# Low parts of attention's query and key weights from a negated cast and an accumulating DMA

## The chip, the cores and the metric

The kernel runs on one core of one Trainium2 chip. The metric is the device time of one execution in microseconds (us). Three runs of the kernel before took 949.86, 948.94 and 949.84 us, a median of 949.84 us. The profile is one further execution; its times count from the start of its span.

Engine names in the profile: PE is TensorE (matrix multiplications), PEld its weight loads, DVE is VectorE, ACT is ScalarE, POOL is GpSimd, SP is SyncE, which issues most of the loads here.

## What is computed

A decoder trunk of two layers on 512 tokens of 1024 features in float32. Layer 0 mixes tokens by pooling, layer 1 by causal differential attention; each is followed by a gated feed-forward network, and a normalisation stands behind every part:

```python
for i in range(DEPTH):
    if i % N_MIXERS == 0:
        h = _multiscale_pool(x, pool_w[j], pool_scale[j])
    else:
        h = _diff_attention(x, w_qkv[j], w_o[j], lam_p[j], subln_g[j], rel_table, lambda_init)
    x = _layernorm(ALPHA * x + h, ln_mix_g[i], ln_mix_b[i])
    x = _layernorm(ALPHA * x + _swiglu(x, w_gate[i], w_up[i], w_down[i]), ln_ffn_g[i], ln_ffn_b[i])
```

The change lies in the attention of layer 1, which has eight heads of two 64-wide halves:

```python
qkv = x @ w_qkv
...
s = jnp.einsum('bhcqd,bhckd->bhcqk', q[...], k[...]) * sm_scale
...
p = jax.nn.softmax(s, axis=-1)
a = p[:, :, 0] - lam * p[:, :, 1]
outs.append(jnp.einsum('bhqk,bhkv->bhqv', a, v[...]))
```

## The kernel before

**Two parts for each operand.** TensorE multiplies in a format called fp32r, which keeps fewer bits than float32. So each operand is held as two tiles: a high part h, the value cast to fp32r, and a low part l, the value minus h. A product takes three multiplications: high by high, high by low, low by high (`mm3`, line 125). `split` (line 102) makes the two parts: a cast on ACT (line 109) and a subtraction on DVE (line 110), or on POOL where the caller asks for it.

**The weight stream.** All weights lie in one array `wall` in HBM, cut into pieces of 128x1024 float32 (512 KB) in the order in which they are used. `fetch` (line 95) has SP load a piece into one of five buffers, `raw`. `ready(upto)` (line 112) brings the stream forward: for each next piece c it first asks for the loads up to piece c + 4, then takes a pair of tiles `w{c}h`, `w{c}l` out of six pairs and splits `raw` into them. The load of piece c + 4 reuses the buffer of piece c - 1, so it waits until nobody reads that one any more. `weights` and `take` hand finished pairs to the multiplications.

**The attention pieces.** Pieces 68 to 91 belong to queries, keys and values. Every pair of heads has six: two of values (`v`, 68 and 69 for heads 0 and 1), then query and key of the even head (70, 71), then query and key of the odd head (72, 73). So w76 and w77 are query and key of head 2, w78 and w79 of head 3, w82 and w83 of head 4, w88 and w89 of head 6. Pieces 92 to 99 are the output projection.

**The order of a head.** The order of all work is written out by hand (line 241): each engine runs its instructions in the order of the program, and waits only for data and for buffers to be free. Head h goes as follows (lines 1183 to 1231). TensorE makes the values (`values`); DVE finishes the previous head's softmax (`combine`, lines 1104 to 1109); `ready` splits pieces up to this head's key; the values are split into `vh`, `vl`; an earlier head's output is scaled (`root`, `scaled`). Then `ready` moves one piece on, TensorE makes the queries, ACT and DVE split them (`heads`, lines 104 and 105), TensorE transposes the previous head's probabilities and makes the keys; `ready` moves on, the keys are split (lines 109 and 110), `ready` moves on again, and `mix` multiplies the previous head's probabilities by its values. ACT squares that result (`sq`, line 1145) and casts the square; POOL subtracts (`sql`). Last come the four score blocks (line 1085), for each of which DVE adds the bias and takes the minimum (line 1090, an accumulator read follows) and ACT takes the exponential (line 1095). The scores are done by TensorE in one go; the next head's values follow them.

So a piece that `ready` splits is, on ACT and DVE, queued between the instructions of the head that calls it: in the odd heads 1, 3 and 5 the query piece of the next head is the last thing before `sq` on ACT and before line 1090 on DVE; in head 0 the key piece of head 1 (w73) and a value piece (w74) are. The key pieces of heads 2, 4 and 6 are split at the start of their own head.

**DMA queues.** SP issues the loads of the weight stream. POOL issues none in attention; in the feed-forward stages it issues plain loads (line 665) and loads that add to what is in the destination (line 666, `accum_op`).

Of the kernel before, what the change touches and what calls it, by code (L numbers as in the profile page):

```python
# [13 lines left out]
F32R = mybir.dt.float32r  # L14
BF16 = mybir.dt.bfloat16
AF = mybir.ActivationFunctionType
ALU = mybir.AluOpType
# [8 lines left out]
FB = FF // P  # L26
HEADS = 8
# [27 lines left out]
def trunk(ctx, tc, x, wall, pscale, lam_p, subln, table, lng, lnb, band, first, onehot, out):  # L55
    nc = tc.nc
# [18 lines left out]
    def weight_pair(name):  # L75
        return tuple(
            keep.tile([P, 1024], F32R, tag=f"w{q}", name=f"{name}{q}", bufs=WBUFS) for q in "hl"
        )
# [11 lines left out]
    raws = {}  # L90
    fetched = [0]
    divided = [0]
    total = wall.shape[0]

    def fetch(upto):
        while fetched[0] < min(upto, total):
            c = fetched[0]
            raws[c] = keep.tile([P, 1024], F32, tag="raw", name=f"raw{c}", bufs=RAWS)
            nc.sync.dma_start(out=raws[c], in_=wall[c])
            fetched[0] += 1  # L100

    def split(dst_h, dst_l, src, scale=1.0, low=None):
        if scale != 1.0:
            nc.scalar.mul(dst_h, src, scale)
            nc.vector.scalar_tensor_tensor(
                dst_l, src, scale, dst_h.bitcast(F32), op0=ALU.mult, op1=ALU.subtract
            )
        else:
            nc.scalar.copy(dst_h, src)  # L109
            (low or nc.vector).tensor_tensor(dst_l, src, dst_h.bitcast(F32), op=ALU.subtract)  # L110

    def ready(upto, low=None):
        while divided[0] < min(upto, total):
            c = divided[0]
            fetch(c + RAWS)
            h, l = weight_pair(f"w{c}")
            split(h, l, raws.pop(c), low=low)
            parts[c] = (h, l)
            divided[0] += 1

    def weights(c):
        ready(c + 1)
        return parts[c]
# [118 lines left out]
    with tc.tile_pool(name="pool", bufs=1) as pp:  # L242
# [161 lines left out]
        mixed(0, 1)  # L404
        mixed(1, 0, 1)
        ready(3, nc.gpsimd)
        summed(0, 0)
        split_pooled(1, 0, 1)
# [24 lines left out]
        spread_of(0, 2)  # L433
        turned(0, 1)
        ready(4)
        summed(3, 0, 1)
        norm(0, 2)
# [939 lines left out]
```

## Time and profile before

| what | value |
|---|---|
| median of three runs | 949.84 us (948.94 to 949.86) |
| span of the profiled execution | 947.3 us |
| that execution's own time | not given apart from its span |
| attention in the span | about 383 to 600 us |
| TensorE's granted clock in attention | 1.00 |
| one key or query piece: cast on ACT, subtraction on DVE | 1.05 us, 1.22 us |

How to read the lines that follow. A row of the timeline gives the start and length in us, the engine, the line of the kernel, the operation, what it writes and reads with shapes, and in brackets how long the engine stood idle before it and what ended that. A row of the waits view gives who waited for whom, the total in us, how often, and the longest. A row by tile or line gives the count, the shortest, median and longest time of one in ns, and the first and last start in us. The row of a window gives its length, then busy time (and count) of PE, PEld, DVE, ACT and POOL, then the granted clock, the busy share of the DMA engines and GB/s. The chain row gives the share of the span by engine in the chain of work that ended last.

### The profile page before, as it was taken

Reading aid. Unit: us, or ns where it says so; the run is one execution under the profiler, and the core shown is the slowest. Engines: PE = TensorE matmul, PEld = TensorE weight load, DVE = VectorE, ACT = ScalarE, POOL = GpSimd, SP = SyncE. Lnnn points to the kernel's source line nnn. Section 1 sums busy time; section 2 is a strip of 40 time slices with the busy share of each in tenths; the row PEclk is TensorE's granted clock in tenths of the full one; section 3 lists DMA queues with packets and bytes.
Section 4 is the critical chain, followed back from the end, with each engine's and each line's share of the span. In section 5 each row is a group of like instructions: output and inputs, shape, how many; then the busy total and the mean of one; then the engine's idle time right before and its main releaser. Section 6 shows DMA issues by size and latency. Waiting matters only on the chain.

```text
span 947.3 us, 15363 instructions
## 1 busy us (share of the span) xinstructions
PE 934.1 (99%) x5976; PEld 845.7 (89%) x5976; DVE 781.3 (82%) x1149; ACT 490.1 (52%) x788; POOL 108.4 (11%) x133
## 2 busy tenths in 40 slices
PE   9999999999999999999999999999999999999996
PEld 8898899999988888988888888998899999988885
DVE  8859879999988777688777677789779999987778
ACT  6752444555564457655566553833345554564450
POOL 4121121110001101000000000211111110001101
PEclk9999999999999999999999999999999999999998
DMA  9387988885888964333233222396888885878952
GB/s 244 125 266 236 341 269 246 265 261 208 255 255 271 363 219 136 95 89 101 78 123 83 64 90 90 118 324 197 262 266 250 255 272 204 261 249 271 356 171 90
DMA packets 82248, 196.99 MB, mean 208 GB/s; under 512 B 14804, under 2 KB 26324, under 8 KB 82174
## 3 DMA queue, kind: packets, MB, share of 16 engines
q1 hardware_dynamic: 42876, 115.07, 36.9%
q0 software_dynamic: 15520, 46.14, 17.8%
q10 hardware_dynamic: 23778, 34.78, 10.2%
q8 instruction: 47, 0.77, 0.3%
q14 instruction: 27, 0.22, 0.1%
HBM read 159.25 MB, written 36.72 MB: 207 GB/s over the span
## 4 chain that ended last, share of the span: by engine, by line
PE 92%; DVE 4%; ACT 2%; issue 1%; POOL 0%; DVEq 0%; POOLq 0%
PE A L820 17%; PE P L886 13%; PE C L820 9%; PE Q L886 6%; PE B L820 4%; PE g L129 3%; PE u L128 3%; PE u L127 3%; PE u L129 3%; PE g L127 3%; PE g L128 3%; PE s L1085 2%; PE v L127 2%; PE v L128 2%; PE v L129 2%; PE q L128 2%
## 5 line engine op out<-in xcount | busy, mean ns | idle before, releaser
L566 DVE TENSOR_TENSOR raw<-raw,raw 128x1024 f32<-128x1024 f32 x56 | 68.3, 1219 | 0.5
L109 ACT CAST xs<-hid 128x512 fp32r<-128x512 f32 (+1 forms) x60 | 34.7, 581 | 24.4 <-DVE hid L734 24.4
L224 ACT ACTIVATE y<-pt,bT,gT 128x128 f32<-128x128 f32 x96 | 36.1, 456 | 20.1 <-PE pt L213 20.1
L110 DVE TENSOR_TENSOR xs<-hid,xs 128x512 fp32r<-128x512 f32 (+1 forms) x60 | 38.5, 644 | 7.8 <-ACT xs L109 7.8
L1095 ACT ACTIVATE p<-p,mn 128x128 f32<-128x128 f32 (+3 forms) x64 | 35.4, 554 | 14.9 <-DVE mn L1090 14.9
L665 POOL DMA_DIRECT2D b<-in_wall x20 | 14.0, 705 | 175.0 <-DVE g_58l L572 66.1
L598 DVE TENSOR_TENSOR hid<-sg,u 128x512 f32<-128x512 f32 x16 | 11.0, 687 | 27.5 <-PE u L129 16.8
L726 POOL DMA_DIRECT2D xs<-ssum x24 | 17.4, 725 | 140.7 <-PE Q L886 119.5
L177 POOL TENSOR_TENSOR rs<-rs,mhalf 128x1 f32<-128x1 f32 x16 | 12.5, 784 | 170.5 <-DVE rs L176 131.0
L110 DVE TENSOR_TENSOR xt<-y,xt 128x512 fp32r<-128x512 f32 x24 | 16.3, 689 | 17.5 <-ACT xt L109 17.5
L1090 DVE CUSTOM_DVE_ANT_0 p<-s,bias 128x128 f32<-128x128 f32 (+3 forms) x64 | 28.1, 485 | 0.0
L665 POOL DMA_DIRECT2D hid<-in_wall x24 | 18.7, 821 | 81.1 <-DMA tsum<-hid 49.4
L110 POOL TENSOR_TENSOR sql<-sq,sqh 128x512 fp32r<-128x512 f32 x7 | 9.0, 1291 | 165.3 <-ACT sqh L109 165.3
L702 ACT CAST v<-u 128x512 fp32r<-128x512 f32 x22 | 13.6, 620 | 26.9 <-DVE u L700 26.7
L168 DVE BATCH_NORM_STATS2 st<-res 128x6 f32<-128x512 f32 x32 | 22.2, 695 | 1.1
L846 ACT ACTIVATE sg<-sg 128x512 f32<-128x512 f32 x14 | 8.9, 633 | 25.7 <-DVE sg L839 25.7
L110 DVE TENSOR_TENSOR heads<-k,heads 128x512 fp32r<-128x512 f32 x8 | 5.5, 692 | 19.9 <-ACT heads L109 19.9
L614 ACT CAST xs<-hid 128x1024 fp32r<-128x1024 f32 x8 | 8.4, 1051 | 24.0 <-DVE hid L631 11.6
L666 POOL DMA_DIRECT2D hid<-in_wall x12 | 14.8, 1232 | 48.2 <-DMA hid<-in_wall 44.9
L835 DVE TENSOR_TENSOR hid<-C,hid 128x512 f32<-128x512 f32 x14 | 9.7, 692 | 10.8 <-PE C L820 9.2
L1109 DVE SCALAR_TENSOR_TENSOR p<-p,sm,p 128x128 f32<-128x128 f32 (+3 forms) x32 | 17.7, 552 | 1.1
L109 ACT CAST heads<-k 128x512 fp32r<-128x512 f32 x8 | 4.7, 589 | 26.0 <-PE k L129 26.0
(1119 smaller groups left out, 3727.7 us busy)
## 6 DMA issues: line engine op xcount, KB each, us to landing
raw<-in_wall SPq DMA_DIRECT2D x122, 512.0 KB, 4.5
r<-tsum SPq DMA_DIRECT2D x40, 512.0 KB, 4.3
hid<-in_wall POOLq DMA_DIRECT2D x36, 512.0 KB, 6.9
b<-in_wall POOLq DMA_DIRECT2D x30, 512.0 KB, 6.4
r<-in_wall SPq DMA_DIRECT2D x30, 512.0 KB, 4.5
tsum<-hid ACTq DMA_DIRECT2D x24, 512.0 KB, 5.3
ssum<-v ACTq DMA_DIRECT2D x22, 512.0 KB, 4.4
tsum<-b ACTq DMA_DIRECT2D x20, 512.0 KB, 5.2
```

The source lines that it names most:

```text
L109: nc.scalar.copy(dst_h, src)
L110: (low or nc.vector).tensor_tensor(dst_l, src, dst_h.bitcast(F32), op=ALU.subtract)
L127: nc.tensor.matmul(acc, ah, bh, start=start, stop=False)
L128: nc.tensor.matmul(acc, ah, bl, start=False, stop=False)
L129: nc.tensor.matmul(acc, al, bh, start=False, stop=stop)
L224: nc.scalar.activation(y[:, k, :], pt[:, k * P : (k + 1) * P], AF.Identity, bias=bT[:, n, kk : kk + 1], scale=gT[:, n, kk : kk + 1],)
L566: tt(t, raws[pair[0]], raws[pair[1]], op=ALU.add)
L665: nc.gpsimd.dma_start(out=t[:, j], in_=src[:, j])
L820: nc.tensor.matmul(o, w[:, c], x[:, kk, :], start=p in ("P1", "Q5", "P2") and f + kk + e == 0, stop=p in ("Q4", "Q3", "P2") and (f, kk, e) ...
L886: nc.tensor.matmul(accs[s], x[:, k, r], y[:, c], start=first and k == 0 and e == 0, stop=last and k == m - 1 and e == 2, skip_group_check= ...
L1090: nc.vector.tensor_tensor_reduce(out=p, in0=accs[c][:, :w], in1=biases[h][:, w - 1 :: -1] if w < S else biases[h][:, ::-1], op0=ALU.add, o ...
L1095: nc.scalar.activation(p, p, AF.Exp, bias=mn[:, q, c : c + 1], scale=-1.0, accum_out=sm[:, q, c : c + 1],)
```

## The change

For the query and key pieces of heads 1 to 7 (14 pieces: 72, 73, 76 to 79, 82 to 85, 88 to 91) the low part is made in another way. ACT casts the raw piece to the high tile as before; then ACT writes the negated cast of the raw piece into the low tile; then POOL issues a DMA that reads the same piece from `wall` in HBM once more and adds it to the low tile. The result is again the value minus its high part. DVE does nothing for these pieces. All other pieces go through `split` as before.

```diff
+    attn = 2 + 3 * FB
+    by_dma = {attn + 6 * (h // 2) + 2 + 2 * (h % 2) + i for h in range(1, HEADS) for i in range(2)}
...
             h, l = weight_pair(f"w{c}")
-            split(h, l, raws.pop(c), low=low)
+            raw = raws.pop(c)
+            if c in by_dma:
+                nc.scalar.copy(h, raw)
+                nc.scalar.mul(l, raw, -1.0)
+                nc.gpsimd.dma_start(out=l, in_=wall[c].bitcast(F32R), accum_op=ALU.add)
+            else:
+                split(h, l, raw, low=low)
             parts[c] = (h, l)
```

## The prediction, made before the changed kernel was run

> **What bounds the kernel now.** I read the page's totals first, then the chain that ended last, then the attention stage alone (383 to 600 us from the span's start: one row of the windows view, then the waits inside it).
>
> ```profile
> span 947.3 us, 15363 instructions
> PE 934.1 (99%) x5976; PEld 845.7 (89%) x5976; DVE 781.3 (82%) x1149; ACT 490.1 (52%) x788; POOL 108.4 (11%) x133
> PE 92%; DVE 4%; ACT 2%; issue 1%; POOL 0%; DVEq 0%; POOLq 0%
> ```
> ```profile
> 383.00:600.00 217.00, 216.77 (x1335) 188.92 (x1334) 163.68 (x360) 124.44 (x274) 10.52 (x9) 1.00 0.29 89
> ```
> ```profile
> ACT heads L109 <- PE k L129: 26.0, 8, 3.8
> ...
> PEld v L127 <- DVE mn L1090: 2.1, 6, 0.4
> ```
>
> TensorE carries 92% of the chain. In attention (the columns are length, then busy time of PE, PEld, DVE, ACT, POOL, then granted clock, DMA share, GB/s) it is busy for 216.8 of 217 us at clock 1.00, DVE for 75%, ACT for 57%, and the DMA engines for 29%. So time taken from DVE is worth only what TensorE waits for DVE here: six waits, 2.1 us together, each for the accumulator read of the fourth softmax pass (line 1090) behind a head's scores. More can be lost: every operand that arrives late stops an engine that now hardly stops.
>
> **What the change removes.** For 14 pieces (query and key, heads 1 to 7) the subtraction on DVE goes: 14 x 1.23 us = 17.2 us (row 415.03 below), taking DVE in this stage from 163.7 to 146.5 us. The prices are in these rows of head 1 and the start of head 2 (engine ACT, then DVE, then PEld, each in order of time):
>
> ```profile
> 413.94 1.05 ACT L109 CAST w76h<-raw 128x1024 fp32r<-128x1024 f32 x1
> 415.33 0.60 ACT L1145 ACTIVATE sq<-o 128x512 f32<-128x512 f32 x1 [0.33 <-PE o L129]
> ...
> 422.49 1.03 ACT L109 CAST w77h<-raw 128x1024 fp32r<-128x1024 f32 x1
> 423.44 0.59 ACT L109 CAST vh<-v 128x512 fp32r<-128x512 f32 x1
> ```
> ```profile
> 415.03 1.23 DVE L110 TENSOR_TENSOR w76l<-raw,w76h 128x1024 fp32r<-128x1024 f32 x1 [0.26 <-ACT w76h L109]
> 416.17 0.28 DVE L1090 CUSTOM_DVE_ANT_0 p<-s,bias 128x128 f32<-128x128 f32 x1
> ...
> 417.28 0.08 DVE L1090 DVE_READ_ACCUMULATOR2_ANT mn<- 128x1 f32 x1
> 417.41 0.17 DVE L1104 RECIPROCAL sm<-sm 128x2 f32<-128x2 f32 x1
> ...
> 423.00 0.55 DVE L1105 TENSOR_SCALAR p<-p,sm,nlam 128x512 f32<-128x512 f32 x1
> ```
> ```profile
> 417.40 0.19 PEld L127 LDWEIGHTS v<-w74h,xt 128*128 128x128 f32 x1 [0.35 <-DVE mn L1090]
> ```
>
> In the odd heads 1, 3 and 5 the removed subtraction (w76, w82, w88) stands just ahead of the first softmax pass: it ends at 416.26 and the pass starts at 416.17, when its scores are already being made. Without it the pass waits for its scores alone. The wait behind it is 0.35 us, so the gain per odd head lies between 0 and 0.35; I take 0.3, nearly the whole wait, since DVE would then be free from 414.77 on (415.03 less the 0.26 it stood idle). In the even heads the piece at that place is a value piece, which stays on DVE, so nothing changes there. Gain: 3 x 0.3 = 0.9 us.
>
> **What it adds on ACT.** 14 negated casts of the same shape as the cast ahead of them, 1.05 us each: 14.7 us, ACT 124.4 to 139.1 of 217 us. From start to next start such a cast costs ACT 0.95 us (422.49 to 423.44). Most lie ahead of a wait of ACT for TensorE (26.0 us over eight heads ahead of the key's cast), which hides them; without that cover each would hold what follows it on ACT by 0.95. Behind w76 the cover is short: cast at 413.94, negated cast 414.89 to 415.94, so sq starts at 415.84, not 415.33: 0.5 later. The exponentials behind sq, the reciprocal (417.41) that waits for them, the later softmax passes and with them w77's cast follow 0.5 later. TensorE waits for none of these in this head.
>
> In head 0 there is no cover:
>
> ```profile
> 393.58 1.05 ACT L109 CAST w73h<-raw 128x1024 fp32r<-128x1024 f32 x1
> 394.52 1.05 ACT L109 CAST w74h<-raw 128x1024 fp32r<-128x1024 f32 x1
> ```
> ```profile
> 395.80 1.22 DVE L110 TENSOR_TENSOR w74l<-raw,w74h 128x1024 fp32r<-128x1024 f32 x1
> 396.94 0.28 DVE L1090 CUSTOM_DVE_ANT_0 p<-s,bias 128x128 f32<-128x128 f32 x1
> ...
> 398.05 0.09 DVE L1090 DVE_READ_ACCUMULATOR2_ANT mn<- 128x1 f32 x1
> ```
> ```profile
> 398.18 0.19 PEld L127 LDWEIGHTS v<-w68h,xt 128*128 128x128 f32 x1 [0.37 <-issue]
> ```
>
> The negated cast of w73 goes between the two casts: w74h starts at 395.46 and ends at 396.51, and w74's subtraction, freed of w73's ahead of it, still starts only at 396.55, 0.75 later than 395.80. The softmax passes behind it move by as much, and the values' first weight load at 398.18 follows the fourth accumulator read (398.05 + 0.09) as it does in head 1 (417.36, then 417.40). The view puts this wait to issue, but the distance is the same. Loss: 0.75 us, with 0 as its other end should that wait not be DVE's.
>
> **What it adds on POOL and the DMA engines.** 14 accumulating transfers of 512 KB, issued by POOL. Nothing accumulates in attention now, so the landing L is bounded by the transfers of line 666 (accumulating) and line 665 (plain, same size and queue) in the feed-forward stages. First line 666 whole, then its one transfer at 688.4, then line 665; then the DMA share around 688 and where the new ones will run; then the plain loads in attention.
>
> ```profile
> L666 POOL DMA_DIRECT2D hid<-in_wall x12: 1222/1230/1243, 55.1 to 748.6; - x12
> ...
> DMA to landing us min/median/max: 5.8/6.9/10.8
> ```
> ```profile
> L666 POOL DMA_DIRECT2D b<-in_wall x1: 1227/1227/1227, 688.4 to 688.4; - x1
> ...
> DMA to landing us min/median/max: 6.0/6.0/6.0
> ```
> ```profile
> DMA to landing us min/median/max: 4.2/6.4/10.5
> ```
> ```profile
> 688.00:695.00 7.00, 7.00 (x42) 6.20 (x41) 3.98 (x6) 0.72 (x2) 1.23 (x1) 1.00 0.93 261
> ...
> 425.00:431.00 6.00, 6.00 (x34) 5.07 (x33) 5.02 (x7) 2.13 (x4) 0.00 (x0) 1.00 0.24 87
> ```
> ```profile
> raw<-in_wall SPq DMA_DIRECT2D x31, 512.0 KB, 3.6
> ```
>
> L lies between 4.2 (as quick as the quickest plain one) and 10.8 (the slowest accumulating one). The engines are at 0.24 where w77's will run, so I go by the quick end of the accumulating rows, 5.8 to 6.0, and take 6.0: SP's next raw load waits for the same negated cast to free its buffer, so it runs beside the accumulation (3.6 us from issue to landing). POOL's queue: the next instruction behind such a DMA is the subtraction of sql, which waits for ACT anyway and is read a head later; an issue of 1.23 us there costs nothing. Destination and source are fp32r here and f32 in line 666; no row has that form, and the upper end stands for it.
>
> A rule of the Trainium skill (DMA: Bandwidth & Descriptors, Anatomy of one DMA) puts a POOL-issued transfer at 2.0 us plus bytes over 436 GB/s, an estimate of 3.2 us for 512 KB. The rows disagree, 4.2 for the quickest plain and 5.8 for the quickest accumulating one. By the rule nothing below would be late and the sum would be that of the second case.
>
> **What becomes late.** The rows give the first weight load of a low part. The key pieces of the even heads, w77, w83 and w89, are the tight ones, cast at the head's beginning and used some 8 us later; of the other eleven the queries of the same heads, w76 first, have the least time.
>
> ```profile
> L129 PEld LDWEIGHTS q<-xt,w76l x8: 187/188/188, 423.9 to 428.7; 128*128 128x128 f32 x8
> ```
> ```profile
> L129 PEld LDWEIGHTS k<-xt,w77l x8: 187/188/188, 430.5 to 435.3; 128*128 128x128 f32 x8
> ```
> ```profile
> 458.92 1.05 ACT L109 CAST w82h<-raw 128x1024 fp32r<-128x1024 f32 x1
> 460.70 0.60 ACT L1145 ACTIVATE sq<-o 128x512 f32<-128x512 f32 x1 [0.72 <-PE o L129]
> ...
> 467.86 1.03 ACT L109 CAST w83h<-raw 128x1024 fp32r<-128x1024 f32 x1
> ```
> ```profile
> L129 PEld LDWEIGHTS k<-xt,w83l x8: 187/188/188, 475.5 to 480.3; 128*128 128x128 f32 x8
> ```
> ```profile
> 503.92 1.05 ACT L109 CAST w88h<-raw 128x1024 fp32r<-128x1024 f32 x1
> 505.42 0.60 ACT L1145 ACTIVATE sq<-o 128x512 f32<-128x512 f32 x1 [0.45 <-PE o L129]
> ...
> 512.59 1.03 ACT L109 CAST w89h<-raw 128x1024 fp32r<-128x1024 f32 x1
> ```
> ```profile
> L129 PEld LDWEIGHTS k<-xt,w89l x8: 187/187/188, 520.5 to 525.3; 128*128 128x128 f32 x8
> ```
>
> w77: cast at 422.49 + 0.51 = 423.00, negated cast 423.95 to 424.99, POOL issues at 425.04, landing at 431.04, and 0.05 for the semaphore: 431.09. TensorE wants it at 430.5, or 430.2 once it has gained 0.3 ahead: it waits 0.9. w83: sq 0.12 late by the rows of w82, cast at 467.98, negated cast 468.93 to 469.97, landing at 476.07 with the semaphore, wanted at 475.2: 0.9. w89: sq 0.40 late, cast at 512.99, POOL issues at 515.03, landing with the semaphore at 521.08, wanted at 520.2: 0.9. Where L is below 5.1 none waits; above, each waits L - 5.1. w76, issued at 415.99 and wanted at 423.6, is late only if L is over 7.6, and what TensorE waits there the key behind it no longer does, since its own issue does not move. The stall moves everything behind it, so nothing else becomes late.
>
> **Sum**, on the profiled execution: 0.75 + 3 x (0.9 - 0.3) = +2.55 us, span 947.3 to 949.85. The median of the runs shown, 949.84, is 2.54 above the span, and that part stays: **952.4 us**. In general the sum is 0.75 + 3 x (max(0, L - 5.1) - 0.3).
>
> **The rivals.**
>
> *The accumulation lands in time* (L at most 5.1): no stall, 0.75 - 0.9 = -0.15, 949.7. For it: the quickest plain one took 4.2 at the same queue, and attention's DMA engines are mostly idle. Against it: none of 22 accumulating ones took under 5.8.
>
> *The accumulation is slow* (fp32r destination, or the raw load beside it): at L = 8.5, between median and maximum, 0.75 + 3 x 3.1 = +10, 959.9; at 10.8, 966.8. For it: the accumulations at 6.9 and above stood beside other loads, as these will. Against it: the share of 0.24.
>
> *DVE's relief decides, and it is faster.* Place: the waits behind the scores. Were all six of them to vanish (2.1 us) and head 0's 0.37 as well, -2.5, 947.3. It decides only if L is under 5.1 and head 0's values do not wait for w74; against it stands that three of the six have a value piece ahead, which the change leaves on DVE.
>
> A rule of the Trainium skill speaks against the change (SBUF — State Buffer, Who interferes with whom): while DVE runs a `tensor_scalar` in its two-port mode, POOL cannot write the descriptors of its DMAs. Were each of the three late transfers to meet the longest such instruction here (line 1105, 0.55 us), the sum would be 3 x 0.55 higher, 954.0. I leave it out: moved by the same 0.5, that instruction ends at 424.06, a microsecond before POOL issues, and the 22 issues of line 666 kept to about 1.23 us.
>
> **How the numbers follow.** The forecast (L from 5.2 to 7.0) has 0.47, with its own range 950.0 to 955.4; in time 0.20; slow 0.26; faster 0.07. Below 948.9 only the faster case lies; the slow case reaches 961 at L = 8.9, above which I leave some 0.1. Range 948.9 to 961. A measurement of this kernel tells about 0.2% from no change, 1.9 us: faster 0.07; within, the second case and the forecast's share with L under 5.8, 0.29; slower 0.64.
>
> **What would show it.** Right: in the changed trace TensorE waits for a DMA at the low parts w77l, w83l and w89l by some 0.9 us each; head 0's wait behind the scores grows from 0.37 to 1.1; the waits of heads 1, 3 and 5 shrink to under 0.1; ACT's sq of head 1 starts later than TensorE's o allows; accumulating landings near 6.0. Wrong: landings under 5 or over 8, waits at query pieces (then L is over 7.6), TensorE waiting for ACT at the scores, or a difference outside 383 to 560 us.

## The result, and the profile after

The changed kernel took 955.0 us (median of four, 954.39 to 956.14) where the kernel before, beside it, took 949.7: a ratio of 1.006, 95% interval 1.0045 to 1.0074, or 5.3 us more. The forecast was 952.4 us, in a range of 948.9 to 961, and slower with a chance of 0.64. The direction held, and so did three of the four places; the size that was forecast was half of what came. The two profiled executions are 6.3 us apart (spans of 947.3 and 953.6 us), 1 us more than the medians. A ratio here is taken over all the runs, so it need not be the quotient of the two medians.

First the totals and the chain of the changed kernel's page, then its attention stage in one row of the windows view (columns as before).

```profile
span 953.6 us, 15383 instructions
...
PE 935.9 (98%) x5976; PEld 846.1 (89%) x5976; DVE 765.7 (80%) x1135; ACT 503.3 (53%) x802; POOL 120.8 (13%) x147
...
PE 86%; DVE 5%; issue 3%; ACT 2%; DMA 2%; POOL 1%; DVEq 0%; POOLq 0%; ACTq 0%
```
```profile
383.00:600.00 217.00, 212.29 (x1311) 184.15 (x1310) 142.98 (x341) 132.63 (x278) 22.72 (x23) 1.00 0.47 121
```

DVE's busy time in the span fell by 15.6 us, as it was meant to (781.3 to 765.7), ACT's rose by 13.2. TensorE, busy for 216.8 us of this stage before, is now busy for 212.3 of the same 217: the stage has got holes. DMA stands in the chain for the first time, with 2%. Where the holes are, the waits view of the changed kernel from 383 to 560 us tells (who waited for whom, total, times, longest):

```profile
DVE p L1098 <- PE s L1093: 3.4, 3, 1.2
...
PEld k L137 <- DMA w89l<-in_wall: 2.8, 1, 2.8
...
PEld v L135 <- DVE mn L1098: 2.2, 6, 0.4
...
PEld k L137 <- DMA w77l<-in_wall: 1.6, 1, 1.6
...
PEld k L137 <- DMA w83l<-in_wall: 1.0, 1, 1.0
...
PEld s L1093 <- DVE mn L1098: 0.8, 1, 0.8
```

Four waits are new: the key pieces w77l, w83l and w89l, 5.4 us together, and head 0's scores, 0.8. That is 6.2 of the 6.3 us between the two spans. The three keys are where the prediction had them; in head 0 it had the wait at the values. The six waits at v (2.2 us) stand as they stood before (2.1). Line numbers are 8 higher from `weights` on; line 122 is the negated cast, line 123 the accumulating DMA.

The landings in the same stage of the changed kernel (issues view, the last column is the median us from issue to landing):

```profile
raw<-in_wall SPq DMA_DIRECT2D x30, 512.0 KB, 4.2
...
w77l<-in_wall POOLq DMA_DIRECT2D x1, 512.0 KB, 6.6
...
w83l<-in_wall POOLq DMA_DIRECT2D x1, 512.0 KB, 6.1
...
w89l<-in_wall POOLq DMA_DIRECT2D x1, 512.0 KB, 7.9
```

Before the change a raw load landed after 3.6 us here, now after 4.2: beside the new transfers the raw loads are slower.

How one of these pieces goes, in the timelines of ACT, POOL and PEld of the changed kernel:

```profile
425.45 1.05 ACT L122 ACTIVATE w77l<-raw 128x1024 fp32r<-128x1024 f32 x1
```
```profile
426.80 0.88 POOL L123 DMA_DIRECT2D w77l<-in_wall  x1 [6.83 <-ACT w77l L122]
```
```profile
431.71 0.19 PEld L136 LDWEIGHTS k<-xt,w77h 128*128 128x128 f32 x1
433.46 0.19 PEld L137 LDWEIGHTS k<-xt,w77l 128*128 128x128 f32 x1 [1.55 <-DMA w77l<-in_wall]
```

The negated cast ends at 426.50, POOL issues 0.30 later, the transfer lands 6.6 after that at 433.4, and the first weight load that needs it starts at 433.46, having been due at 431.91.

### The profile page after: what moved, and what is told of

The parts are those of the page before. It is cut to its first block, busy times and chain, and to the rows that moved or that the text cites. A ratio compares the mean times of both kernels' runs of the same rounds, so it can differ in the third digit from the quotient of the medians.

```text
span 953.6 us, 15383 instructions
## 1 busy us (share of the span) xinstructions
PE 935.9 (98%) x5976; PEld 846.1 (89%) x5976; DVE 765.7 (80%) x1135; ACT 503.3 (53%) x802; POOL 120.8 (13%) x147
## 4 chain that ended last, share of the span: by engine, by line
PE 86%; DVE 5%; issue 3%; ACT 2%; DMA 2%; POOL 1%; DVEq 0%; POOLq 0%; ACTq 0%
PE A L828 17%; PE P L894 13%; PE C L828 8%; PE Q L894 6%; PE B L828 4%; PE g L137 3%; PE u L136 3%; PE u L135 3%; PE u L137 3%; PE g L136 3%; PE g L135 3%; PE k L137 2%; PE k L135 1%; PE k L136 1%; PE s L1093 1%
## 5 line engine op out<-in xcount | busy, mean ns | idle before, releaser
L1103 ACT ACTIVATE p<-p,mn 128x128 f32<-128x128 f32 (+3 forms) x64 | 35.4, 555 | 14.7 <-DVE mn L1098 14.7
L1093 PE MATMUL s<-heads 64*128 64x256 f32 (+2 forms) x192 | 18.2, 330 | 0.4 <-DVE mn L1098 0.4
L843 DVE TENSOR_TENSOR hid<-C,hid 128x512 f32<-128x512 f32 x14 | 9.7, 691 | 10.8 <-PE C L828 9.3
```

Source lines behind the costliest of these rows:

```text
L1103: nc.scalar.activation(p, p, AF.Exp, bias=mn[:, q, c : c + 1], scale=-1.0, accum_out=sm[:, q, c : c + 1],)
```

## The experiments

Theory A: three key pieces arrive late and head 0's scores wait behind w74; the other ten pieces cost nothing. Rival B: the loss is spread over all 14, by more DMA traffic and more work on ACT. Within A it was open why the landing takes so long: the raw load that starts beside it (A1), the accumulation by itself (A2), or HBM as its source (A3). Each experiment starts from the changed kernel; each was timed beside the kernel before, and "above" means above its median in the same set of runs.

### Which pieces cost the time

**Without the three key pieces.**

```diff
+    by_dma -= {77, 83, 89}
```

> The low parts of w77, w83 and w89 go back to the DVE subtraction; the other eleven pieces stay with the accumulating DMA. Theory A (three low parts arrive late, and head 0's scores wait behind w74): no wait of TensorE for a DMA in attention, head 0's wait of 0.8 us stays, time 0.5 to 1.0 us above before (ratio 1.0005 to 1.001). Rival B (the loss is spread over all 14 pieces: more DMA traffic, more ACT work): eleven fourteenths of 5.3 us stay, 4.2 us above before (1.0044).

Measured 950.7 us, 1.3 above (ratio 1.0012, 1.0003 to 1.0021). No wait at a key piece is left, head 0's 0.8 stays, and w76l is waited for by 0.2. B's 4.2 us are excluded; A's figure was 0.3 too low.

**The three key pieces alone.**

```diff
-    by_dma = {...}
+    by_dma = {77, 83, 89}
```

> Only w77, w83 and w89 are made by negated cast and accumulating DMA. Theory A: the query pieces no longer push ACT back by 0.5, 0.1 and 0.4 us, so the three waits shrink by about that and sum to some 4 us, time 3.5 to 4.5 us above before (1.004). Rival B: three fourteenths of 5.3 us, 1.1 us above before (1.0012).

Measured 952.47 us, 3.1 above (1.0031, 1.0019 to 1.0042): 0.4 below A's window, far above B's 1.1. These are the waits of this kernel:

```profile
PEld k L137 <- DMA w89l<-in_wall: 1.8, 1, 1.8
...
PEld k L137 <- DMA w83l<-in_wall: 0.8, 1, 0.8
PEld k L137 <- DMA w77l<-in_wall: 0.4, 1, 0.4
```

They sum to 3.0 us, as the time does. Against the changed kernel's 1.6, 1.0 and 2.8 they are shorter, because ACT is not pushed back by the query pieces' negated casts: from POOL's issue to the moment at which TensorE wants the piece there are 5.7, 5.6 and 5.6 us here, and 5.1, 5.1 and 5.2 in the changed kernel. The landing of w77l (6.06 us for 6.61) and of w89l (7.4 for 7.9) is shorter too, that of w83l is not (6.4 for 6.1).

**Without w73, and w73 alone.**

```diff
+    by_dma -= {73}
```

> Only w73 goes back to the DVE subtraction. Theory A: head 0's wait of 0.8 us at the scores vanishes and the three waits at w77l, w83l, w89l stay (1.6, 1.0 and 2.8 us in the changed kernel's profile), time 4.3 to 4.8 us above before (1.0045 to 1.005). Rival B: thirteen fourteenths of 5.3 us, 4.9 us above before, and the wait in head 0 stays as well.

Measured 955.89 us, 6.5 above (1.0068, 1.0055 to 1.0081): a miss in the time. In its profile head 0's wait is gone, as A has it, but the three waits came out at 1.2, 1.8 and 2.7 us, 5.7 in place of 5.3, and five runs from 954.98 to 958.06 don't resolve 0.8 us. The run of 958.06 us has the lowest mean granted clock of all the runs here, 0.995 where the others have 0.996 to 0.998, so a drop of the clock like the one at the end of this section may be part of the miss; that run was not profiled. So the reverse was run:

```diff
-    by_dma = {...}
+    by_dma = {73}
```

> Only w73 is made by negated cast and accumulating DMA. Theory A: head 0's wait at the scores alone, 0.8 us in the profile, time 0.5 to 0.9 us above before (1.0005 to 1.001). Rival (the wait in head 0 is hidden again later): within 0.2 us of before.

Measured 950.18 us, 0.75 above (1.0005, 0.9997 to 1.0014). The profile shows head 0's wait of 0.8 us and no other new one. The size is as expected, though the interval reaches 1.

**The other ten alone.**

```diff
+    by_dma -= {73, 77, 83, 89}
```

> w73, w77, w83 and w89 go back to DVE; ten pieces stay with the accumulating DMA. Theory A: nothing is late, no wait of TensorE for a DMA, head 0 as before, time within 0.3 us of before (1.000). Rival B (spread): ten fourteenths of 5.3 us, 3.8 us above. A rival that DVE's relief is worth something where nothing is late: 0.5 to 1 us below before (0.999).

Measured 949.7 us, 0.5 above (1.0008, 0.9999 to 1.0017). No gain from DVE's relief, and B's 3.8 us are excluded. A wait of 0.2 us at w76l is the one new one; the rest of the 0.5 is below what these runs tell.

**ACT's part alone.**

```diff
                 nc.scalar.mul(l, raw, -1.0)
-                nc.gpsimd.dma_start(out=l, in_=wall[c].bitcast(F32R), accum_op=ALU.add)
```

> All 14 negated casts stay and the accumulating DMAs are left out, so the low part of these pieces holds minus the high part and the output is not the reference's. Theory A: only head 0's wait remains, 0.5 to 1.0 us above before (1.0005 to 1.001). A rival that puts the loss on ACT (negated casts delaying what follows): the loss stays near 5 us. A rival that expects a gain from DVE's relief once nothing is late: 1 to 2 us below before plus head 0's 0.8.

Measured 950.06 us, 0.7 above (1.0004, 0.9995 to 1.0013). Of TensorE's waits only head 0's is new:

```profile
PEld s L1092 <- DVE mn L1097: 0.8, 1, 0.8
```

So 13 us more on ACT are by themselves hidden except at that one place, and the rest of the loss comes only with the transfers.

### Why the landing is long

**The raw tile as source.** The buffer stays taken until the accumulation has landed, so no raw load can start into it beside that.

```diff
-                nc.gpsimd.dma_start(out=l, in_=wall[c].bitcast(F32R), accum_op=ALU.add)
+                nc.gpsimd.dma_start(out=l, in_=raw.bitcast(F32R), accum_op=ALU.add)
```

> The accumulating DMA reads the raw tile in SBUF in place of the weights in HBM, so the raw buffer comes free only when it has landed and SP's next load cannot run beside it. Theory A1 (the raw load beside it delays the accumulation): landing 5.0 to 5.8 us in place of 6.1 to 8.8, waits at the three keys shrink to 0 to 0.5 us each, time 0.7 to 2 us above before. Theory A2 (the accumulation is slow by itself, some 2.75 us of every DMA engine and a fixed part): landing stays at 6 or more, waits of 1 us or more each, 4 us or more above before.

Measured 951.0 us, 1.8 above (1.0018, 1.0009 to 1.0027). The landings, in the issues view of this kernel:

```profile
w77l<-raw POOLq DMA_DIRECT2D x1, 512.0 KB, 4.5
...
w83l<-raw POOLq DMA_DIRECT2D x1, 512.0 KB, 4.5
...
w89l<-raw POOLq DMA_DIRECT2D x1, 512.0 KB, 5.6
```

Only w89l is still waited for, by 0.4. A2 as it was put falls: an undisturbed accumulation into the same tile lands in 4.5 us. But two things were changed at once, the neighbour and the source.

**The raw loads moved, the source left in HBM.** ACT issues them at their place in the program, so they no longer start the moment the negated cast frees the buffer.

```diff
-            nc.sync.dma_start(out=raws[c], in_=wall[c])
+            (nc.scalar if 76 <= c < 96 else nc.sync).dma_start(out=raws[c], in_=wall[c])
```

> As the changed kernel, but the raw loads of pieces 76 to 95 are issued by ACT at their place in the program, so the load that reuses a buffer no longer starts as soon as the negated cast has freed it, beside the accumulation. The source of the accumulation stays in HBM. Theory A1 (the raw load beside it holds the accumulation's packets back by 1.2 to 1.5 us): first packet of w77l, w83l and w89l after about 1.5 us and landing 4.5 to 5.5, waits 0 to 0.5 us each, time 0.7 to 2 us above before, as with the raw tile as source. Theory A3 (reading HBM in place of SBUF makes the difference): landing stays over 6 us, time 4 us or more above before.

Measured 951.1 us, 1.7 above (1.0018, 1.0009 to 1.0026), less than the waits in its profile: head 0's has grown to 1.3, because ACT now issues a load (0.33 us) ahead of the cast of w74, and w77l is waited for by 0.2, w89l by 0.7. The landings in this kernel:

```profile
w77l<-in_wall POOLq DMA_DIRECT2D x1, 512.0 KB, 5.3
...
w83l<-in_wall POOLq DMA_DIRECT2D x1, 512.0 KB, 5.1
...
w89l<-in_wall POOLq DMA_DIRECT2D x1, 512.0 KB, 5.8
```

For w77l and w83l HBM as source costs some 0.7 us (5.2 against 4.5), the raw load beside it the rest. The packets of these transfers, taken from the traces one by one, show at which end:

```
us after POOL's issue      first packet  last packet ends  lands
w77l, changed kernel           2.97           6.32          6.61
w77l, loads moved              1.59           4.99          5.29
w77l, raw tile as source       1.44           4.21          4.50
w83l, changed kernel           2.82           5.83          6.12
w83l, loads moved              1.61           4.83          5.13
w83l, raw tile as source       1.44           4.21          4.51
```

The raw load holds back the first packet by 1.2 to 1.4 us. A1 holds for w77l and w83l, and A3 falls; w89l landed after 5.8 and was waited for by 0.7, beyond A1's 5.5 and 0.5.

**A copy in place of the accumulation.** The low part is then the whole value.

```diff
-                nc.gpsimd.dma_start(out=l, in_=wall[c].bitcast(F32R), accum_op=ALU.add)
+                nc.gpsimd.dma_start(out=l, in_=wall[c].bitcast(F32R))
```

> The DMA of the 14 pieces copies the weights over the low tile in place of adding to it (all else, the negated cast and POOL's issue too, as in the changed kernel), so the low part is the whole value and the output is not the reference's. If the accumulation's double engine time (0.33 us for 4 KB where a plain packet takes 0.16) makes the landing long: landing 4.2 to 5.5 us, waits at the three keys 0 to 0.3 us, time 0.7 to 1.5 us above before. If the POOL queue and the raw load beside it make it long: landing over 6 us and waits of 0.7 us or more each, 3 us or more above.

Measured 950.64 us, 1.4 above (1.0014, 1.0005 to 1.0023). All fourteen landings of this kernel, by line 123:

```profile
DMA to landing us min/median/max: 4.3/4.6/5.8
```

The first packet of w77l and w83l still comes 2.6 us after the issue, held back much as before (3.0 and 2.8); what is saved lies behind it, with 2.0 and 1.6 us from the first packet to the end of the last one, where the changed kernel took 3.4 and 3.0. So the double engine time of the accumulation (a 4 KB packet takes 0.33 us where a plain one takes 0.16) is a second cause beside the raw load: taking away either one brings w77l and w83l in time, but for the 0.2 left at w77l with the loads moved. w89l is waited for even here, by 0.7, where 0 to 0.3 was expected.

### Taking every wait away

**The key pieces split earlier**, in the odd head before, ahead of its first softmax combination.

```diff
-                if h == HEADS - 1:
+                if h % 2:
                     ready(where[0] + 4)
```

> The key piece of the next even head (w77, w83, w89) is split in the odd head before, ahead of its first softmax combination, some 5 us earlier than in the changed kernel; all 14 pieces stay with the accumulating DMA. Theory A: the landing keeps its 6 to 9 us but is in time, no wait at the three keys, time 0.5 to 1.3 us above before (head 0's wait, and up to 0.4 for ACT's exponentials that now come later). Rival B: 5 us above before, as in the changed kernel.

Measured 950.23 us, 1.0 above (1.0010, 1.0001 to 1.0019), with head 0's wait and 0.2 at w76l and none at the keys, although the median landing of its fourteen transfers is 7.1 us. The three keys themselves landed sooner than expected, after 5.8, 5.1 and 6.0 us, with the raw load now issued 1.6 us behind them and no longer 0.3 ahead. At the old place, with some 5.1 us from issue to need, two of them would still have come an estimated 0.7 and 0.9 too late. So the hour of the issue matters here, but it was not the only thing that changed; the next version settles it.

**Everything at once**: raw tile as source, keys early, w73 back on DVE.

> Thirteen pieces keep the accumulating DMA; it reads the raw tile, the key pieces of the even heads are split a head's end earlier, and w73 goes back to DVE: every wait named so far is taken away at once. Theory A: no wait of TensorE beyond those of before, time within 0.4 us of before (1.000); DVE's 16 us less busy time buys nothing. Rival (DVE's relief is worth something once nothing else is late): 1 us or more below before (0.999 or less).

Measured 950.03 us, 0.6 above (1.0004, 0.9995 to 1.0013). Its key pieces took about as long to land as those of the changed kernel (6.6, 6.1 and 7.9), and TensorE waits for none of them:

```profile
w77l<-raw POOLq DMA_DIRECT2D x1, 512.0 KB, 7.7
...
w83l<-raw POOLq DMA_DIRECT2D x1, 512.0 KB, 6.4
...
w89l<-raw POOLq DMA_DIRECT2D x1, 512.0 KB, 6.4
```

At the old place each would have come an estimated 1.3 to 2.7 us too late. What cost the time was the hour of the issue against that of the use. The waits of TensorE from 383 to 560 us in this kernel are those of before, one by one:

```profile
PEld v L136 <- DVE mn L1099: 2.2, 6, 0.4
PEld q L137 <- DVE xt L113: 0.4, 1, 0.4
PEld v L136 <- issue: 0.4, 1, 0.4
PEld wo L136 <- DVE mn L1099: 0.4, 1, 0.4
```

With all lateness taken away, 13 subtractions fewer on DVE buy nothing that can be measured. No version was found that beats the kernel before.

**The changed kernel once more.**

> The changed kernel once more, beside the others. All theories: 4.5 to 6 us above before (1.005 to 1.006); by A the waits at w77l and w83l 0.9 to 1.8 us and the one at w89l the longest, over 2 us, since a 16 KB instruction fetch falls into its transfer each time.

Measured 956.12 us, 6.7 above (1.0065, 1.0051 to 1.0078), a little beyond the 4.5 to 6 expected. The waits at the keys were 1.5, 1.7 and 2.7 us. What else happened shows in two windows of this profile and in PE's timeline behind the wait for w89l:

```profile
526.80:531.20 4.40, 4.40 (x13) 3.52 (x14) 0.00 (x0) 0.50 (x1) 0.85 (x1) 0.63 0.92 216
531.20:535.00 3.80, 3.80 (x20) 3.23 (x19) 0.69 (x1) 1.32 (x2) 0.00 (x0) 0.98 0.90 218
```
```profile
526.74 0.50 PE L137 MATMUL k<-xt,w89l 128*128 128x512 f32 x1 [2.25 <-DMA w89l<-in_wall]
...
528.45 0.63 PE L137 MATMUL k<-xt,w89l 128*128 128x512 f32 x1
528.87 0.63 PE L135 MATMUL k<-xt,w89h 128*128 128x512 f32 x1
...
531.64 0.40 PE L136 MATMUL k<-xt,w89h 128*128 128x512 f32 x1
531.88 0.39 PE L137 MATMUL k<-xt,w89l 128*128 128x512 f32 x1
```

The granted clock is 0.63 in the stretch behind the wait; for 3.4 us of it, from 528.0 to 531.4, it is 0.50. From 528.0 to 531.0 the multiplications start 0.43 us apart in place of 0.23. Seven of them at 0.2 us more are 1.4 us that the wait itself does not show.

## Why the prediction was right or wrong

**What bounds the kernel** was right: TensorE alone. The version with every wait taken away shows it best. Against the prediction's own sum, DVE had not even 0.9 us to give.

**DVE's relief, -0.9 us**, was wrong. The step "the wait behind it is 0.35 us, so the gain per odd head lies between 0 and 0.35; I take 0.3" took the view's releaser for the cause. Head 1 of the changed kernel, DVE first, then PEld:

```profile
417.38 0.29 DVE L1098 CUSTOM_DVE_ANT_0 p<-s,bias 128x128 f32<-128x128 f32 x1 [1.10 <-PE s L1093]
...
418.49 0.08 DVE L1098 DVE_READ_ACCUMULATOR2_ANT mn<- 128x1 f32 x1
```
```profile
416.72 1.78 PEld L1093 LDWEIGHTS s<-heads 64*128 64x128 f32 x24
418.85 0.19 PEld L135 LDWEIGHTS v<-w74h,xt 128*128 128x128 f32 x1 [0.36 <-DVE mn L1098]
```

DVE did become free (it now waits 1.1 us for the scores) and its fourth read ends at 418.57, 0.28 ahead of the weight load, where before it was 0.04 ahead. The gap stayed at 0.36, and it is 0.35 to 0.37 at every head of every profile here, whatever DVE did. So it is hardly a wait for DVE; that TensorE's own last score multiplications set its length is inferred from its sameness, and no run changed them. From the first score weight load to the values' it was 2.18 us before and is 2.13 now: the gain was 0.05, the low end of the range given.

**ACT's 14.7 us** were nearly right. By themselves they are hidden but for head 0, as the run without transfers shows; but they push back the issue of the keys by 0.4 to 0.6 us each (the three keys alone, above), where the prediction had 0.5, 0.1 and 0.4. ACT's busy time rose by 13.2 us and DVE's fell by 15.6, not by 14.7 and 17.2: rows behind each other overlap, so one counts from its start to the next start (0.95 us on ACT).

**Head 0, +0.75**, was right in size (0.75 us with w73 alone; counted from the start of w73's cast, DVE's subtraction of w74 began 2.98 us later where it was 2.22) and wrong in its place. Not the values but the last five weight loads of the scores wait, by the view for the accumulator read of the first softmax pass, which ends at 398.72, 0.06 ahead of them; that this pass frees the bank which they write is inferred. The values' wait stayed at 0.37, where the prediction had it grow to 1.1. The rows are ACT's, DVE's and PEld's of the changed kernel:

```profile
394.31 1.05 ACT L121 CAST w73h<-raw 128x1024 fp32r<-128x1024 f32 x1
395.26 1.06 ACT L122 ACTIVATE w73l<-raw 128x1024 fp32r<-128x1024 f32 x1
396.22 1.03 ACT L111 CAST w74h<-raw 128x1024 fp32r<-128x1024 f32 x1
```
```profile
397.29 1.23 DVE L112 TENSOR_TENSOR w74l<-raw,w74h 128x1024 fp32r<-128x1024 f32 x1 [2.15 <-ACT w74h L111]
398.43 0.28 DVE L1098 CUSTOM_DVE_ANT_0 p<-s,bias 128x128 f32<-128x128 f32 x1
398.64 0.08 DVE L1098 DVE_READ_ACCUMULATOR2_ANT mn<- 128x1 f32 x1
```
```profile
398.78 0.52 PEld L1093 LDWEIGHTS s<-heads 64*128 64x128 f32 x5 [0.82 <-DVE mn L1098]
```

**The late keys, +2.7**, were the right mechanism at the right three pieces, mis-sized by half: 5.3 us at the weight loads. The term "L ... take 6.0" measured 6.6, 6.1 and 7.9; POOL needed 0.25 us more than the 0.05 allowed to wake behind ACT; and the 0.3 "gained ahead" was not there. With these the prediction's own sum gives L - 5.15 for each wait, 1.5, 1.0 and 2.7 us, and the trace has 1.55, 1.01 and 2.76. The choice of 6.0 went by the DMA share of 0.24 and undervalued what the same sentence named: the raw load starts with the accumulation, not at random, so a mean share says little of the moment that counts.

In all seven runs that split these keys at their old place w89l is the longest, by 0.6 to 1.8 us over the other two. In each of them one 16 KB instruction fetch, 0.9 to 1.7 us long, falls between its issue and its landing and none into those of w77l and w83l. A second raw load is a rival: in the changed kernel one is issued 4.8 us behind w89l's issue, where for w77l and w83l none follows within 6.5. With the raw tile as source no load begins within w89l's transfer, only the fetch falls into it, and it was still 1.1 us later than the other two. In the version with every wait taken away no fetch falls into it, and it landed after 6.4 us as w83l did. Both speak for the fetch as a part of it; against it, with the keys early w89l was the last of the three (6.0 us) without a fetch. No run took the fetch alone away, so the cause stays open.

**The bounds.** 4.2 to 10.8 us for L held: 6.1 to 8.8 in the changed kernel. The median of its fourteen landings is 7.9, not "near 6.0", and three lie over 8 (w79l, w73l and w85l), which the prediction had named as a sign of being wrong; none of those three is waited for. The limit of 7.6 for w76l held: in the three runs in which it was waited for, by 0.2, it landed after 7.7 to 7.8 us. The fp32r form, for which the upper end stood, cost nothing that could be seen: the undisturbed accumulation landed in 4.5 us from SBUF and 5.1 to 5.3 from HBM, quicker than any f32 one of before (5.8, in rows of 2 KB). An f32 destination was not tried.

**The rivals.** Landing in time was not the case at the keys; where the version with every wait taken away made it so, with w73 back on DVE, the time was 0.6 us above before, with an interval that takes in no change. The faster case never came. POOL's issues show no sign of being held up by DVE: the fourteen took 0.85 to 0.92 us each. By the Trainium skill (DMA: Bandwidth & Descriptors, Anatomy of one DMA) 512 KB from POOL would take an estimated 3.2 us; the copies took 4.3 to 5.8, the accumulations 4.5 to 9.6 over all the runs, so the measurements decide against it here.

## What to carry to other kernels

A busy share says whether an engine can be relieved, not whether that is worth anything: read the waits of the bounding engine, and doubt one that has the same length everywhere. A result that moves from an engine to a DMA is ready only when the transfer has landed, in the changed kernel 6 to 9 us after its issue, so list its uses and compare each with the new time of readiness; here three of fourteen were short and carried most of the loss. The transfer that starts at the same event as yours counts more than the mean DMA share.

## What the runs showed of the hardware

- An accumulating transfer of 512 KB takes twice the engine time of a plain one (0.33 against 0.16 us for a 4 KB packet). Undisturbed it lands after 4.5 us from SBUF and some 5.2 from HBM; with a plain load issued 0.3 us ahead of it, w77l and w83l landed after 6.1 to 6.9 from HBM.
- POOL issued a DMA of 4 KB rows that accumulates in 0.85 to 0.93 us, where line 666, with 2 KB rows, took 1.23.
- TensorE's granted clock fell to half for 3.4 us, behind a wait of 2.25 us between multiplications, in one of three profiles with such a wait (2.25 to 2.33 us; two are of the changed kernel, one of the version without w73). The one in which it fell had the shortest of the three. The Trainium skill (TensorE: Matmul & The Clock Gate, Part 1) has the clock halve after an idle window of about 3.4 us. The half rate agrees with the trace (0.43 for 0.23 us between starts); in that one profile a shorter wait was enough.
